# A decoder trunk on one core: the attention's matmuls in the order of the source, forget logits by token, gate biases on another queue

## The chip, the cores and the metric

The kernel runs on one core of a Trainium2 chip. The metric is the device time of one execution in microseconds, as a median over several runs. The engines that matter here: PE (TensorE, matmuls and transposes, with PEld for its weight loads), DVE (VectorE), ACT (ScalarE), POOL (GpSimd) and SP (SyncE, which does no arithmetic here and issues nearly all transfers). PSUM holds what PE writes.

## The reference

The inputs are x (256 tokens x 1024, float32), a conditioning vector c and the parameters. There are two layers. Layer 0 mixes tokens with an S5 state space, layer 1 with attention that has a forget gate per head; each is followed by a mixture of experts (32 experts in 4 groups, the top 2 of one group). Every part begins with an RMS norm and a shift and a gain worked out from c, and is added back through a gate worked out from c:

```python
def shared_kv(x, c, ...):                  # after layer 0
    h = modulate(rmsnorm(x, kv_g), shift, scale)
    k, v, fz = jnp.split(h @ kv_w, [D_MODEL, 2 * D_MODEL], axis=-1)   # fz: 16 forget logits a token
    k = rmsnorm(k.reshape(bsz, seq, N_HEADS, HEAD_DIM), k_norm_g).transpose(0, 2, 1, 3)
    logf = jax.nn.log_sigmoid(fz + kv_fb)
    fcum = jnp.cumsum(logf, axis=1).transpose(0, 2, 1)

def fox_mixer(h, w_qg, q_norm_g, w_o, k, v, fcum):
    q, og = jnp.split(h @ w_qg, 2, axis=-1)          # og: the output gate
    q = rmsnorm(q ...)
    logits = einsum(qb, kb) * scale + fcum[:, :, s0:s1, None] - fcum[:, :, None, :s1]
    p = softmax(where(causal mask, logits, NEG))     # in two blocks of 128 queries
    return (o * jax.nn.sigmoid(og)) @ w_o

# layer l:  h = h + gate * mix(...);  h = h + gate * hier_moe(...)
```

## The kernel before

**Stages.** The S5 layer runs until about 206 us, the experts of layer 0 (MoE0) until 424, the attention until about 640, and the experts of layer 1 (MoE1) to the end at 852. All weights are float32 and come from memory once, in blocks of 1 MB (128 partitions x 2048). `block` takes a block, and `prefetch` issues transfers ahead of use into a ring of slots, in an order that the source sets; a block is issued on SP's queue when the slot's last reader is done. In the attention the ring has 12 slots; `release` and the end of the values add 3 and 4 slots out of memory that the heads gave up, and MoE1's first blocks are fetched into all 19 (`ahead_of_moe`, `load`).

**Projections.** k, v and q are projections of the normed and modulated x (`hn_parts`: 16 transposes L1156, shift and gain on ACT and DVE into xf, then xf split into a hi and a lo part). A weight block of 512 columns is split likewise (`split_next`: hi on ACT at L1128, lo on DVE at L1129, tile ws, three buffers). `project` does six matmuls per quarter (hi x hi, lo x hi, hi x lo for two token halves, L1199), 48 per projection; a run of two gives k, v or q. `out_gate` (L1393, 12 a quarter, 192 in all) forms the output gate and `out_proj` (L1430, 96) the output.

**Fillers.** Shift, gain and gate for the attention are worked out from c by PE (`ada_cols_pe`, L169; `ada_gate_pe`, L184 and L194) and those for MoE1 by DVE (`ada_cols_v`, L214, one pass over 128 x 1024 at a time), in pieces that the source places between projections. POOL multiplies wo by the gate (L1126, 16 times).

**Heads.** They go in four groups. `turned_heads` transposes k and q (L1291); `weights` forms the logits of 128 queries, then of the other 128 (L1316), adds the mask and takes the maximum on DVE (L1319), negates it (L1323), takes the exponent on ACT (L1325), the reciprocal of the sum (L1327), and multiplies (L1328); `turned_weights` transposes the weights (L1342); `values` multiplies by v (L1409, L1412). These are generators, which `tick` advances between quarters.

**Forget gates.** `forget_logits` (L1189) forms the logits as 16 x 256 (head by token); `forget_gates` adds the bias, turns them by two transposes (L1243) into 128 x 32, and goes on with log-sigmoid and cumulative sum.

**Order.** The framework's scheduler orders each engine's instructions by its own costs, so PE's program isn't the source's. Each engine executes its row in order. A wait on PE holds what stands behind it.

**Lines that the change touches:** L181 (gate biases), L535 to L589 (`overflow`, which is entered only when an expert has more tokens than its tile, which isn't so with these inputs), L1173 on (the attention), L1189 and L1238 on (forget logits and gates), L1480 (the end of the attention).

Of the kernel before, what the change touches and what calls it, by code (L numbers as in the profile page):

```python
# [21 lines left out]
KD = 8  # L22
# [12 lines left out]
C_RB, C_LRE, C_LIM, C_LDT, C_GB, C_S5D, C_N = 140, 212, 244, 276, 308, 340, 356  # L35
# [3 lines left out]
def trunk(ctx: ExitStack, tc: tile.TileContext, A, out, ring=12, ring2=4, ring3=5, ring4=3, ring5=4, lpb=2, TK=2):  # L39
# [135 lines left out]
    def ada_gate_pe(name, j, li, gbc, at_once=False):  # L175
# [4 lines left out]
        for n in range(2):  # L180
            nc.scalar.dma_start(rows[32 * n:32 * n + 1, :], A["gbias"][li, n:n + 1, :])  # L181
# [150 lines left out]
    def moe(l, sh, g, gbc, c36, slots_):  # L332
# [200 lines left out]
        def overflow(rv):  # L533

            with tc.If(rv > CAP):  # L535
# [15 lines left out]
                with tc.For_i(0, NQ, 1) as q:  # L551
                    gcol = t2("gcol", 4)
                    G.dma_start(gcol, gov.rearrange("p i (q s) -> p i q s", s=4)[:, :, bass.ds(q, 1), :]
                                      .rearrange("p i o s -> p i (o s)"))
                    for s in range(4):
                        c = slice(512 * s, 512 * s + 512)

                        def part(name, j):
                            w = mb[0].tile([128, 2, 512], F32, tag="ow", name="ow", bufs=1)
                            G.dma_start(w, A[name][l, bass.ds(q, 1), 2 * j:2 * j + 2, :, c]  # L560
                                              .rearrange("o k p n -> p (o k) n"))
                            return w

                        ph = [mm_tile() for _ in range(2)]
                        for kp in range(4):
                            w = part("wa", kp)
                            for i in range(2):
                                for kk in range(2):
                                    PE.matmul(ph[i], hnT[i][:, 2 * kp + kk, :], w[:, kk],
                                              start=kp + kk == 0, stop=kp == 3 and kk == 1)  # L570
                        aTs = []
                        for i in range(2):
                            a = mb[0].tile([128, 256], F32, tag="a", name="oa", bufs=2)
                            S.activation(a, ph[i][:, 0:256], AF.Silu)
                            V.scalar_tensor_tensor(a, a, gcol[:, i, s:s + 1], ph[i][:, 256:512],
                                                   op0=OP.mult, op1=OP.mult)
                            aTs.append(turned(a))
# [1043 lines left out]
```

## Time and profile before

| what | value |
| --- | --- |
| median of 3 runs (lowest, highest) | 849.39 us (849.17, 849.5) |
| profiled execution: time, span | 854.14 us, 852.5 us |
| mean granted clock of PE | 0.941 |
| busy: PE, DVE, ACT, POOL | 722.5 (85%), 410.1 (48%), 218.3 (26%), 58.3 (7%) us |
| moved from memory | 297.31 MB, mean 350 GB/s with what is written |
| chain that ended last, by engine | PE 47%, DMA 31%, DVE 17%, ACT 2%, issue 2% |

Busy time is an average over stages with different limits: the experts' stages move weights at about 419 GB/s without a pause, while the attention is limited by what its engines do. A row in time gives the start, the length of a group of like instructions (a float32 matmul leaves two records, and some records can be missing, so xcount is a count of records), the operation with its tiles, and in brackets the idle time of the engine before it with what ended it. Lengths of neighbouring PE rows overlap a little, since matmuls are pipelined.

### The profile page before, as it was taken

How to read it: one execution, taken by the hardware profiler on the slowest of the kernel's cores; microseconds unless marked ns; L12 is line 12 of the kernel's file. 1: busy time of each engine (PE TensorE's matmuls, PEld its weight loads, DVE VectorE, ACT ScalarE, POOL GpSimd, SP SyncE). 2: the span in 40 equal slices, each digit the busy share in tenths (PEclk: the TensorE clock that was granted, in tenths of full speed). 3: DMA queues.
4: the chain of work that ended last, by engine and by line, in shares of the span. 5: the costliest groups of instructions: out<-in, count | busy, mean ns of one | idle time of the engine just before them, and what ended most of it. 6: DMA issues, size and time to landing. Idle time of an engine off the chain costs nothing.

```text
span 852.5 us, 13440 instructions
## 1 busy us (share of the span) xinstructions
PE 722.5 (85%) x5382; PEld 401.3 (47%) x5382; DVE 410.1 (48%) x1069; ACT 218.3 (26%) x498; POOL 58.3 (7%) x52
## 2 busy tenths in 40 slices
PE   2777999898899997576799999899998999887766
PEld 0655776575533333131255567788755334331311
DVE  6657799875322322120355569997553223221102
ACT  4323233162300110010232255556522001100100
POOL 2000000000000000000001202870000000000000
PEclk9988999998999999889799999999989999997898
DMA  9996856687999999999999787552679999999996
GB/s 365 416 420 256 328 218 248 264 344 289 419 420 418 421 418 419 420 416 421 420 418 399 282 324 260 196 188 100 241 306 394 419 419 419 418 419 419 418 418 247
DMA packets 41830, 299.32 MB, mean 351 GB/s; under 512 B 4632, under 2 KB 4760, under 8 KB 5664
## 3 DMA queue, kind: packets, MB, share of 16 engines
q1 hardware_dynamic: 41328, 297.13, 86.3%
q10 hardware_dynamic: 432, 1.25, 0.4%
q8 instruction: 45, 0.74, 0.4%
q14 instruction: 25, 0.20, 0.1%
HBM read 297.31 MB, written 1.05 MB: 350 GB/s over the span
## 4 chain that ended last, share of the span: by engine, by line
PE 47%; DMA 31%; DVE 17%; ACT 2%; issue 2%; POOL 0%; SPq 0%; ACTq 0%; DVEq 0%; POOLq 0%
DMA w<-wa 14%; DMA w<-wb 10%; PE mm L506 8%; PE acc L1199 7%; PE mm L470 5%; PE mm L521 4%; PE acc L528 4%; PE acc L1430 3%; DVE m L921 2%; DMA w<-win 2%; DVE m L935 2%; DMA w<-ada00g 2%; PE mm L169 2%; DMA w<-ada 2%; DVE m L954 2%; PE acc L1393 2%
## 5 line engine op out<-in xcount | busy, mean ns | idle before, releaser
L506 PE MATMUL mm<-w,xg 128*32 128x512 f32 x1024 | 140.0, 637 | 33.6 <-DMA w<-wa 22.7
L506 PEld LDWEIGHTS mm<-w,xg 128*32 128x32 f32 x1024 | 29.4, 111 | 118.3 <-issue 69.1
L521 PE MATMUL mm<-w,aT 128*32 128x512 f32 x512 | 68.4, 650 | 12.1 <-DMA w<-wb 6.3
L1199 PE MATMUL acc<-ws,hn 128*128 128x512 f32 x288 | 77.7, 409 | 0.7 <-DVE ws L1129 0.7
L478 ACT ACTIVATE xg<-mm,sh,g 128x128 f32<-128x128 f32 x64 | 29.3, 457 | 187.0 <-PE mm L470 170.9
L1129 DVE TENSOR_TENSOR ws<-w,ws 128x512 fp32r<-128x512 f32 x80 | 60.7, 768 | 32.7 <-ACT ws L1128 32.5
L470 PE MATMUL mm<-Pr,h 128*128 128x128 f32 x512 | 64.9, 280 | 11.0 <-DVE Pr L458 11.0
L470 PEld LDWEIGHTS mm<-Pr,h 128*128 128x128 f32 x512 | 60.5, 193 | 26.4 <-issue 23.2
L528 PE MATMUL acc<-y,Sc 128*128 128x512 f32 x128 | 64.7, 629 | 6.5 <-DVE y L524 5.7
L1128 ACT ACTIVATE ws<-w 128x512 fp32r<-128x512 f32 x80 | 49.7, 629 | 67.9 <-PE acc L1199 49.5
L476 DVE TENSOR_SCALAR xg<-mm,g,sh 128x128 f32<-128x128 f32 x64 | 26.2, 410 | 75.2 <-ACT xg L478 75.2
L1199 PEld LDWEIGHTS acc<-ws,hn 128*128 128x128 f32 x288 | 51.1, 188 | 23.9 <-issue 7.1
L524 DVE TENSOR_TENSOR y<-mm,gbc 128x512 f32<-128x512 f32 x32 | 22.1, 692 | 67.6 <-PE mm L521 67.3
L489 DVE COPY Sc<-mm 128x256 f32<-128x256 f32 x16 | 6.8, 425 | 86.0 <-PE mm L487 86.0
L511 ACT ACTIVATE a<-mm 128x256 f32<-128x256 f32 x16 | 6.1, 383 | 163.7 <-PE mm L506 163.7
L528 PEld LDWEIGHTS acc<-y,Sc 128*128 128x128 f32 x128 | 22.2, 193 | 45.9 <-issue 28.7
L512 DVE TENSOR_TENSOR a<-a,mm 128x256 f32<-128x256 f32 x16 | 6.7, 419 | 76.9 <-ACT a L511 76.9
L521 PEld LDWEIGHTS mm<-w,aT 128*32 128x32 f32 x512 | 14.1, 114 | 53.6 <-issue 35.4
L984 PE MATMUL acc<-w,uT 128*128 128x512 f32 x64 | 31.7, 642 | 5.7 <-ACT uT L973 5.7
L808 PE MATMUL mm<-hnT,w 128*64 128x128 f32 x512 | 33.3, 291 | 2.7 <-ACT hnT L275 2.7
L1393 PE MATMUL acc<-hn,ws 128*128 128x256 f32 x192 | 29.4, 310 | 5.2 <-DVE ws L1129 5.2
L808 PEld LDWEIGHTS mm<-hnT,w 128*64 128x64 f32 x512 | 31.4, 143 | 4.5 <-ACT hnT L275 3.7
(337 smaller groups left out, 1004.2 us busy)
## 6 DMA issues: line engine op xcount, KB each, us to landing
w<-wa SPq DMA_DIRECT2D x128, 1024.0 KB, 19.9
w<-wb SPq DMA_DIRECT2D x64, 1024.0 KB, 19.9
w<-ada SPq DMA_DIRECT2D x36, 1024.0 KB, 8.8
w<-ada00s SPq DMA_DIRECT2D x8, 1024.0 KB, 18.0
w<-kvada SPq DMA_DIRECT2D x8, 1024.0 KB, 9.1
w<-win SPq DMA_DIRECT2D x4, 1024.0 KB, 18.5
w<-ada00g SPq DMA_DIRECT2D x4, 1024.0 KB, 18.9
w<-woutv SPq DMA_DIRECT2D x4, 1024.0 KB, 17.4
```

The costliest lines, as they stand in the source:

```text
L470: PE.matmul(px[:, 128 * c4:128 * c4 + 128], h[:, i, 128 * c:128 * c + 128], Pr[:, i].rearrange("p a b -> p (a b)"), start=i == 0, stop=i == 1)
L476: V.tensor_scalar(xg[:, c], src, g[:, c:c + 1], sh[:, c:c + 1], op0=OP.mult, op1=OP.add)
L478: S.activation(xg[:, c], src, AF.Identity, bias=sh[:, c:c + 1], scale=g[:, c:c + 1])
L506: PE.matmul(ph[32 * s:32 * s + 32, :], xg[:, k, 32 * s:32 * s + 32], w[:, 512 * s:512 * s + 512], start=k == 0, stop=k == KD - 1)
L521: PE.matmul(py[32 * s:32 * s + 32, :], aT[:, 128 * f + 32 * s:128 * f + 32 * s + 32], w[:, 512 * s:512 * s + 512], start=f == 0, stop=f == 1)
L528: PE.matmul(acc[i][n], scs[q][:, 128 * i:128 * i + 128], y[:, 512 * n:512 * n + 512], start=q == 0, stop=q == NQ - 1, skip_group_check=True)
L808: PE.matmul(ps[64 * v:64 * v + 64, 128 * hh:128 * hh + 128], w[:, k, c0:c0 + 64], hnT[:, k, v::2], start=k == 0 and hh == 0, stop=k == KD ...
L984: PE.matmul(val[t][n], uT[:, m, 128 * t:128 * t + 128], wval[m // 2][:, c0:c0 + 512], start=m == 0, stop=m == 7)
L1128: S.activation(o[:, 0], w, AF.Copy)
L1129: V.tensor_tensor(o[:, 1], w, o[:, 0].bitcast(F32), op=OP.subtract)
L1199: PE.matmul(pk[i], src[:, k, a, 128 * i:128 * i + 128], w[:, b], start=k + a + b == 0, stop=k == KD - 1 and b == 1)
L1393: PE.matmul(po[:, 256 * m2:256 * m2 + 256], w[:, bb, kk, 128 * m2:128 * m2 + 128], hq[:, k, a, :], start=k + a + bb + m2 == 0, stop=k == K ...
```

## The change

1. In `ada_gate_pe` the two transfers of the gate's bias (2 KB each, four gates) are issued by SP and not by ACT.
2. From the norm of x for k and v to the end of the attention PE's instructions keep the order of the source (`manual_schedule`); the other engines' rows are still the scheduler's.
3. The forget logits are formed by token: x is the stationary operand (128 x 128) and the 16 columns of weights the moving one, 16 matmuls for 8 before. The result is 128 x 32 at once; zT, the two transposes and a copy go, and the bias comes as 32 columns.
4. `overflow` has a second hardware loop in place of a Python loop over four quarters; its weights come by SP, its gates are shifted by two copies. The scratch for dynamic transfers is 1024 and not 2048.

```diff
@@ ada_gate_pe
-            nc.scalar.dma_start(rows[32 * n:32 * n + 1, :], A["gbias"][li, n:n + 1, :])
+            nc.sync.dma_start(rows[32 * n:32 * n + 1, :], A["gbias"][li, n:n + 1, :])
@@ overflow
-                with tc.For_i(0, NQ, 1) as q:
-                    gcol = t2("gcol", 4)
-                    G.dma_start(gcol, ...)
-                    for s in range(4):
-                        c = slice(512 * s, 512 * s + 512)
+                gnext = t2("gnext", NE)
+                with tc.For_i(0, NQ, 1) as q, tc.For_i(0, 2048, 512) as c:
...
+                    V.tensor_copy(gnext[:, :, 0:NE - 1], gov[:, :, 1:NE])
+                    V.tensor_copy(gov[:, :, 0:NE - 1], gnext[:, :, 0:NE - 1])
...
@@ the attention
+    in_order = ExitStack()
+    in_order.enter_context(tc.manual_schedule(engines={PE.engine}))
     xs = tp.tile([128, 2, D], F32, tag="xs", name="xs", bufs=1)
@@ forget_logits
-            PE.matmul(pz[:16, :T], smallw[:, k, 0:16], x[:, k2, :], start=k == 0, stop=k == KD - 1)
+            for i in range(2):
+                PE.matmul(pz[:, 16 * i:16 * i + 16], x[:, k2, 128 * i:128 * i + 128], smallw[:, k, 0:16],
+                          start=k + i == 0, stop=k == KD - 1, skip_group_check=True)
@@ forget_gates
-        zT = ap.tile([16, T], F32, name="zT")
-        V.tensor_scalar(zT, pz[:16, :T], cols[:16, C_FB:C_FB + 1], None, op0=OP.add)
-        yield
-        pt = mm_tile()
-        for i in range(2):
-            PE.transpose(pt[:, 16 * i:16 * i + 16], zT[:, 128 * i:128 * i + 128], ident[:16, :16])
...
-        V.tensor_copy(fz, pt[:, :32])
+        V.tensor_tensor(fz, pz[:, 0:32], cols[:, C_FBR:C_FBR + 32], op=OP.add)
@@ end of the attention
     out_proj(3)
+    in_order.close()
     ssq = new_ssq()
...
-    nc = bacc.Bacc("TRN2", target_bir_lowering=False, num_devices=1, dynamic_dma_scratch_size=2048)
+    nc = bacc.Bacc("TRN2", target_bir_lowering=False, num_devices=1, dynamic_dma_scratch_size=1024)
```

Three places of the engines' rows. In the changed kernel L1200 is what L1199 was, L1153 was L1156, L1285 was L1291, L1310 was L1316, L1336 was L1342, L1387 was L1393, L1126 was L1129, L1226 was L1225, L1317 was L1323, L1321 was L1327, L1322 was L1328 and L1409 was L1415; L1189 and L169 keep their numbers. A number x16 counts instructions.

PE where k begins, before (the shift's columns L169, the logits L1189, the projection L1199):

```order
L169 MATMUL mm<-w,sc 32x256 x13
L1189 MATMUL acc<-xf,smallw 16x256
L1199 MATMUL acc<-ws,hn 128x512 x2
L169 MATMUL mm<-w,sc 32x256 x3
L1199 MATMUL acc<-ws,hn 128x512 x5
L1189 MATMUL acc<-xf,smallw 16x256
L1199 MATMUL acc<-ws,hn 128x512 x4
L1189 MATMUL acc<-xf,smallw 16x256
L1199 MATMUL acc<-ws,hn 128x512 x6
L1189 MATMUL acc<-xf,smallw 16x256
L1199 MATMUL acc<-ws,hn 128x512
L1189 MATMUL acc<-xf,smallw 16x256
```

The same place after, from the transposes of x to the cumulative sum of the forget gates (`tri`) and the rest of the fourth projection:

```order
L1153 MATMUL mm<-ident,xs 128x128 x16
L1189 MATMUL acc<-smallw,xf 128x16 x16
L1200 MATMUL acc<-ws,hn 128x512 x48
L169 MATMUL mm<-w,sc 32x256 x32
L1200 MATMUL acc<-ws,hn 128x512 x48
L169 MATMUL mm<-w,sc 32x256 x32
L1200 MATMUL acc<-ws,hn 128x512 x6
L1263 MATMUL mm<-f_z,tri 128x16
L1264 MATMUL mm<-f_z,ones 128x16
L1265 MATMUL mm<-f_z,tri 128x16
L1200 MATMUL acc<-ws,hn 128x512 x42
```

The columns stand in two blocks of 32, each behind 48 projections, where they were spread in pieces between them; the logits stand ahead of the first projection.

PE at the first head group, before, from the logits of the heads (L1316) over the output gate (L1393) to the first turned weights (L1342):

```order
L1316 MATMUL mm<-kA,qA 128x128 x4
L1393 MATMUL acc<-hn,ws 128x256 x2
L1199 MATMUL acc<-ws,hn 128x512 x2
L1393 MATMUL acc<-hn,ws 128x256 x22
L1316 MATMUL mm<-kA,qA 128x256 x4
L1393 MATMUL acc<-hn,ws 128x256 x4
L1291 MATMUL mm<-ident,kn 66x128 x4
L1393 MATMUL acc<-hn,ws 128x256 x48
L1342 MATMUL mm<-ident,pr 128x128 x4
L1291 MATMUL mm<-ident,kn 66x128 x4
```

The same place after (L1310, L1387, L1336):

```order
L1387 MATMUL acc<-hn,ws 128x256 x12
L1310 MATMUL mm<-kA,qA 128x128 x4
L1387 MATMUL acc<-hn,ws 128x256 x12
L1310 MATMUL mm<-kA,qA 128x256 x4
L1387 MATMUL acc<-hn,ws 128x256 x36
L1285 MATMUL mm<-ident,kn 66x128 x4
L1336 MATMUL mm<-ident,pr 128x128 x4
```

Of the output gate's matmuls 76 stood between the first logits and the first turned weights, and now 48; 12 now stand ahead of the logits.

DVE ahead of the first group's multiply by the reciprocal, before (L1328; L214 is a pass over a weight block for MoE1, L1129 the split of a block):

```order
L1221 TENSOR_SCALAR ss<-ss 128x8
L1327 RECIPROCAL sm<-sm 128x4
L214 ISA w,g_111<-w,scr 128x1024
L214 ISA g_111 128x1
L214 ISA w,g_111<-w,scr 128x1024
L214 ISA g_111 128x1
L1129 TENSOR_TENSOR ws<-w,ws 128x512
L1323 TENSOR_SCALAR mx<-mx 128x4
L1328 TENSOR_TENSOR pr<-pr,sm 128x512
```

The same stretch after, up to L1322:

```order
L1317 TENSOR_SCALAR mx<-mx 128x4
L1226 TENSOR_TENSOR qn<-acc,rs 128x8x64
L1126 TENSOR_TENSOR ws<-w,ws 128x512
L1317 TENSOR_SCALAR mx<-mx 128x4
L1409 TENSOR_SCALAR sgT<-sgT 128x512
L1126 TENSOR_TENSOR ws<-w,ws 128x512
L214 ISA w,g_111<-w,scr 128x1024
L214 ISA g_111 128x1
L214 ISA w,g_111<-w,scr 128x1024
L214 ISA g_111 128x1
L1321 RECIPROCAL sm<-sm 128x4
L1126 TENSOR_TENSOR ws<-w,ws 128x512
L217 TENSOR_TENSOR g_111<-g_111,cols 128x8
L1322 TENSOR_TENSOR pr<-pr,sm 128x512
```

The two L1226, which write q's heads, and two more splits stand ahead of the multiply; in before the same L1225 stood behind it.

## Rows read from the trace of the kernel before

**Rows 1.** Windows: from:to, length, busy (instructions) by engine, clock, DMA, GB/s.

```profile
424.00:450.00 26.00, 22.58 (x129) 12.28 (x128) 14.23 (x25) 9.86 (x19) 2.06 (x2) 0.93 1.01 419
...
450.00:480.00 30.00, 30.00 (x148) 15.33 (x147) 18.51 (x61) 9.56 (x17) 4.69 (x4) 1.00 0.88 350
...
480.00:510.00 30.00, 30.00 (x140) 18.60 (x140) 16.52 (x31) 12.15 (x21) 2.86 (x2) 1.00 0.89 326
...
530.00:560.00 30.00, 24.01 (x146) 21.21 (x146) 30.00 (x52) 15.53 (x35) 26.08 (x16) 0.91 0.55 200
```

**Rows 2.** Chain of waits, end of the span: start, length, what.

```profile
732.67 19.89 DMA w<-wb
...
813.80 20.11 DMA w<-wa
```

**Rows 3.** PE in time: start, length, operation, records, idle before.

```profile
428.64 1.97 PE L1156 MATMUL mm<-ident,xs 128*128 128x128 f32 x8 [0.93 <-DVE xs L254]
...
432.12 2.08 PE L169 MATMUL mm<-w,sc 128*32 128x256 f32 x23
...
480.29 1.18 PE L1199 MATMUL acc<-ws,hn 128*128 128x512 f32 x4
...
495.34 1.06 PE L184 MATMUL mm<-w,sc 128*32 128x512 f32 x8
...
515.51 16.11 PE L1199 MATMUL acc<-ws,hn 128*128 128x512 f32 x68
...
626.81 2.77 PE L382 MATMUL acc<-smallw,hT 128*128 128x36 f32 x24
...
633.08 5.22 PE L184 MATMUL acc<-w,sc 128*32 128x512 f32 x32
```

**Rows 4.** Chain of waits, the gate columns before the S5 layer.

```profile
86.08 3.59 PE mm L169 x64
```

**Rows 5.** DVE in time, projections.

```profile
431.21 1.29 DVE L1168 TENSOR_TENSOR hn<-xf,hn 128x512 fp32r<-128x512 f32 x2 [0.24 <-ACT hn L1167]
...
435.27 0.54 DVE L1163 TENSOR_SCALAR xf<-mm,gkv,shkv 128x256 f32<-128x256 f32 x1 [0.66 <-ACT xf L1165]
...
508.75 1.22 DVE L214 CUSTOM_DVE_ANT_0 w<-w,scr 128x1024 f32<-128x1024 f32 x1
```

**Rows 6.** PE in time, head groups.

```profile
536.39 1.06 PE L1316 MATMUL mm<-kA,qA 66*128 66x128 f32 x8
...
538.00 2.77 PE L1393 MATMUL acc<-hn,ws 128*128 128x256 f32 x22
...
540.60 1.89 PE L1316 MATMUL mm<-kA,qA 66*128 66x256 f32 x8
...
546.34 5.57 PE L1393 MATMUL acc<-hn,ws 128*128 128x256 f32 x32 [2.46 <-DVE ws L1129]
...
554.38 0.66 PE L1342 MATMUL mm<-ident,pr 128*128 128x128 f32 x4
...
557.47 6.04 PE L1393 MATMUL acc<-hn,ws 128*128 128x256 f32 x36 [2.00 <-DVE ws L1129]
...
565.21 1.16 PE L1316 MATMUL mm<-kA,qA 66*128 66x128 f32 x8
```

**Rows 7.** DVE in time, head groups.

```profile
531.09 3.31 DVE L1129 TENSOR_TENSOR ws<-w,ws 128x512 fp32r<-128x512 f32 x2
...
553.65 0.68 DVE L1328 TENSOR_TENSOR pr<-pr,sm 128x512 f32<-128x512 f32 x1
...
573.85 0.69 DVE L1328 TENSOR_TENSOR pr<-pr,sm 128x512 f32<-128x512 f32 x1
```

**Rows 8.** POOL in time.

```profile
530.88 14.19 POOL L1126 TENSOR_TENSOR w<-w,gbc 128x512 f32<-128x512 f32 x8
```

**Rows 9.** The tile rows: engine, operation, ns min/median/max, first to last start.

```profile
L179 POOL MEMSET rows<- x4: 524/524/527, 30.0 to 632.3; 128x512 f32 x4
```

**Rows 10.** Waits of the SP queue, 553 to 660 us: total, times, longest.

```profile
SPq L67 <- PE acc L184: 12.7, 3, 11.1
```

More of the change, by code (lines that the diff above doesn't have):

```diff
@@ new lines, in overflow, with part @@
+                with tc.For_i(0, NQ, 1) as q, tc.For_i(0, 2048, 512) as c:
+                    def part(name, j):
+                        w = mb[0].tile([128, 2, 512], F32, tag="ow", name="ow", bufs=1)
+                        nc.sync.dma_start(w, A[name][l, bass.ds(q, 1), 2 * j:2 * j + 2, :, bass.ds(c, 512)]
+                                          .rearrange("o k p n -> p (o k) n"))
+                        return w
+                    ph = [mm_tile() for _ in range(2)]
+                    for kp in range(4):
+                        w = part("wa", kp)
+                        for i in range(2):
+                            for kk in range(2):
+                                PE.matmul(ph[i], hnT[i][:, 2 * kp + kk, :], w[:, kk],
+                                          start=kp + kk == 0, stop=kp == 3 and kk == 1)
+                    aTs = []
+                    for i in range(2):
+                        a = mb[0].tile([128, 256], F32, tag="a", name="oa", bufs=2)
+                        S.activation(a, ph[i][:, 0:256], AF.Silu)
+                        V.scalar_tensor_tensor(a, a, gov[:, i, 0:1], ph[i][:, 256:512], op0=OP.mult, op1=OP.mult)
+                        aTs.append(turned(a))
+                    V.tensor_copy(gnext[:, :, 0:NE - 1], gov[:, :, 1:NE])
+                    V.tensor_copy(gov[:, :, 0:NE - 1], gnext[:, :, 0:NE - 1])
+                    for n in range(2):
+                        w = part("wb", n)
+                        py = [mm_tile() for _ in range(2)]
+                        for f in range(2):
@@ L567, in overflow @@
                             for i in range(2):
[L568 to L571, printed above, removed]
+                                PE.matmul(py[i], aTs[i][:, 128 * f:128 * f + 128], w[:, f],
+                                          start=f == 0, stop=f == 1)
                         for i in range(2):
[L573 to L577, printed above, removed]
@@ L578, in overflow @@
[L578 to L592 removed]
+                            for c2 in range(2):
+                                r = slice(256 * c2, 256 * c2 + 256)
+                                t = mb[0].tile([128, 256], F32, tag="a", name="ot", bufs=2)
+                                V.tensor_tensor(t, py[i][:, r], gbc[:, 512 * n + 256 * c2:512 * n + 256 * c2 + 256],
+                                                op=OP.mult)
+                                PE.matmul(acc[i][n][:, r], ident, t, start=False, stop=False, skip_group_check=True)
@@ L1188, in forget_logits @@
             k = 2 * kk + k2
-            PE.matmul(pz[:16, :T], smallw[:, k, 0:16], x[:, k2, :], start=k == 0, stop=k == KD - 1)
+            for i in range(2):
+                PE.matmul(pz[:, 16 * i:16 * i + 16], x[:, k2, 128 * i:128 * i + 128], smallw[:, k, 0:16],
+                          start=k + i == 0, stop=k == KD - 1, skip_group_check=True)
     hk = hn_parts(xs, shkv, gkv, forget_logits)
@@ L1540, in layouts @@
     cols[:64, C_QG] = fox_q_norm_g[0]
-    for j in range(4):
-        cols[:, C_GB + 8 * j:C_GB + 8 * j + 8] = col(ab[j, 2 * D:])
+    cols[:, C_FBR:C_FBR + 32] = np.tile(np.asarray(kv_fb), 2)[None]
     kvw = np.asarray(kv_w)
```

28 lines of the change are left out of this document (1 added, 27 removed).

## The prediction

> **What bounds the kernel now.** I read the windows first, then the end of the chain of waits, then PE's instructions in time through the attention, and last what DVE and POOL do where PE idles. The end of the span is a stream of weights: five transfers of about 20 us follow each other in the chain until 833.9 us [rows 2], so MoE1 ends when its blocks have landed. A 1 MB block costs about 2.5 us of that stream (eight queue inside one 19.89). Of MoE1's 96 blocks, 19 have slots before it starts; the other 77 x 2.5 = 192 us can only begin when its first matmuls free slots. So a microsecond won or lost ahead of MoE1 is one at the end. What counts is the attention, 424 to 640 us. There PE is busy throughout the projections (30.00 of 30 us in two windows) and DVE is busy throughout 530 to 560, where PE has 24.01 of 30 [rows 1].
>
> **The change part by part.**
>
> *k, v and their fillers.* Before, the 128 records of the shift and gain columns (L169) stand in some 25 pieces between the projections, ends at 480.29 [rows 3]. After, PE does all forget logits, then 48 projections, 32 columns, 48, 32, 48. The bunched form has its own row: 64 records in 3.59 us [rows 4], so 7.2 for both halves. A projection in a long run takes 16.11/68 = 0.237 us [rows 3], so the 108 that before has done by 480.29 take 25.6. The three small matmuls of the cumulative sum add 0.6. The start: the logits now keep the first projection behind the fourth pair of columns of x. DVE formed that pair by 435.27 + 0.54 = 435.8 [rows 5], and the last eight records of the logits come after it at 2.77/24 = 0.115 each (L382 [rows 3]), 0.9 us: 436.7 at the latest. ScalarE's part of it stood behind a run of 23 L169 that began at 432.12 and took 2.08 [rows 3], which is no longer there; at the earliest 435.3. I take 436.0. New wait: DVE does two passes of L214 (1.22 each [rows 5]) ahead of the fifth split, and PE has nothing else in its row by then: up to 2.4, I take 2.3. The end is 436.0 + 25.6 + 7.2 + 0.6 + 2.3 = 471.7 against 480.3: **-8.6**. Bounds: -10 (start at 435.3, half of the wait) to -5 (further waits for ws of 0.2 us on each of 18 splits). The 16 logits themselves are no term: 32 records at 0.115 are 3.7 us, inside the time in which x's columns are formed. The dropped transposes, zT and its copy lie beside other work, worth 0.2 on PE.
>
> *The gate and the second set of transposes.* Six pieces of L184 (1.06 with eight records, some of it under the next operation [rows 3]; I count 1.0) become one bunch; the bunch has a row of 5.22 [rows 3], so 6.0 becomes 5.2, -0.8. The transposes for q, before spread among projections, now stand together ahead of q: PE waits from its last transpose until the first hi and lo exist. For k the transposes ended at 428.64 + 1.97 = 430.6 [rows 3], and DVE had the first two lo parts at 431.21 + 1.29 = 432.5 [rows 5]: 1.3 to 1.9 us for one or both, and with two L214 ahead on DVE 3.7 to 4.3. I take 2.4, nearer to the first since the L214 may be done by then: net **+1.6**, bounds +0.5 to +3.5.
>
> *q.* 96 projections in the same form; DVE has no slack here, more waits on ws: **+0.7**, bounds 0 to +2.5.
>
> *The first head group.* This is the place that decides. In before PE issues the first logits of heads (L1316) at 536.39, and L1342, which turns the weights, at 554.38 [rows 6], because DVE's L1328 runs at 553.65 [rows 7]. In between PE does 76 of the 192 gate projections L1393, and still idles 2.46 us in one piece [rows 6]. After, only 48 stand between the two, and 12 ahead. Cover after: L1316 1.06 and 1.89, 48 x 0.118 = 5.7 (22 in the 2.60 from 538.00 to 540.60), and about 0.5 for four transposes (0.66 for those at 554.38): 9.1 us [rows 6]. DVE's chain was 553.65 + 0.68 - 536.39 = 17.9 us long [rows 6, 7]. PE therefore stands about **9 us in one piece**. Most of it isn't lost against before, since before was held by the same chain; lost is what PE did meanwhile: 16 L1393, 1.9 us. Besides, the order on DVE puts three splits, two L1225 and L214 differently: two L1225 and a split stand ahead of L1328 now that stood behind it, and the backlog of splits and L214 before L1319 is longer; 0 to 5 us, I take 3. Against that, before waited 2.00 at 557.47 for just this work [rows 6], which goes. Net **+2.9**, bounds 0 to +7.
>
> The trace shows POOL's eight multiplies of wo from 530.88 [rows 8], and beside them two splits (L1129) taking 3.31 us [rows 7], where two subtractions of the same size take 1.29 [rows 5]; after, both stand in the same stretch of the order. The Trainium skill (SBUF — State Buffer, Who interferes with whom) says that a DVE instruction with two inputs in SBUF contends with a GpSimd instruction that reads SBUF. By that, the chain is as long in after; without it, the stall would be 2.0 shorter with each such pair.
>
> In the 2.46 us of idle before 546.34 PE waited for ws, and what stands behind in its row waited with it [rows 6]; so nothing behind L1342 fills the 9 us. The Trainium skill (TensorE: Matmul & The Clock Gate, Step-by-step: what each phase is for) says that matmuls stay in program order and only weight loads are pulled ahead. By that the 9 us stay empty, as the row has it; if PE could pass the wait, the sum would be 1.9 us better.
>
> *The other groups.* Group 1: chain from 565.21 [rows 6] to 573.85 + 0.69 [rows 7], 9.3 us; cover in after: 1.1 + 1.9 for L1316, 36 L1393 at 0.118 = 4.2, 1.6 for the values' 16 records (estimated at the 0.1 of small matmuls) and 0.5: 9.3; no stall to speak of. Group 2 has 12 L1393 fewer behind the values, 7.9, so 1.4 if its chain is as long; group 3 has 24 output matmuls at 0.237 and is covered. A part of that was idle before too: **+0.7**, bounds -1 to +4. The granted clock was 0.91 in 530 to 560, where PE idled 6 us [rows 1]; a single longer idle may cost as much again, 0.09 x 30 = 2.7, or nothing: **+0.5**.
>
> *gbias on SP.* The two 2 KB transfers wait for POOL's memset of rows, first at 30.0 and last at 632.3 us [rows 9]. SP's next block in MoE1 waits up to 11.1 us for L184 anyway, which begins at 633.08 [rows 3, 10]. With SP blocked, what it would hold up is the weights behind; about eight blocks are in flight (19.89 for one of 2.5 us [rows 2]). **0**, bounds -0.3 to +2.
>
> *overflow, the scratch size.* The block isn't entered; its branches lie in the end of each MoE, under the DMA stream. **0**, bounds -1 to +1.
>
> Sum: -8.6 + 1.6 + 0.7 + 2.9 + 0.7 + 0.5 = **-2.2**. The profiled execution takes 854.14 us (span 852.5), 4.75 above the median of 849.39; I apply the same difference to both, so 851.9 profiled and **847.2** for the median.
>
> **The rivals.**
>
> *The whole lead stays.* DVE is as far ahead as PE, because its splits are made at PE's pace and the L1225 moved forward aren't missing later. Then the first group costs 0 and the small terms 0: -8.6 + 1.6 = -7.0, with the lower bounds of both -9.5: 842.4 to 839.9. For it: DVE is busy only 18.51 of 30 in the projections [rows 1]. Against it: 30.00 of 30 between 530 and 560.
>
> *Nothing stays: the weights aren't there.* From 424 to 510 the windows move 26 x 419 + 30 x 350 + 30 x 326 = 31.2 MB [rows 1], 74.4 us at 419 GB/s. After has about 79 us for it, so DMA would be at 94%. If blocks come in the wrong order for it, some 2 to 3 us of the lead become waits: -2.2 + 2.5 = +0.3, 848 to 851. Against it: blocks are issued up to 12 slots ahead.
>
> *Slower: each head group stalls.* The mechanism is that of the first group: with PE in source order each chain L1319, exponent, L1328 is covered only by the 7 to 9 us of work that the source places in it. It decides from the point where the chains of groups 1 to 3 average above about 10 us, which needs DVE as late there as in the first group. At 13 us: 3 x 13 - (9.3 + 7.9 + 9.5) = 12 us of stalls, 11 more than counted, and 2 back since the splits are then ready: -2.2 + 9 = +6.8, 856.2. With 11 us each, 33 - 26.7 = 6.3, 5 more than counted, +2.8, 852.2. For it: POOL's second eight multiplies fall beside group 1. Against it: the chain of group 1 is 9.3 us as traced.
>
> **How the numbers follow.** Forecast (842 to 850) 0.52, of which 0.44 lies below 847.7; the whole lead 0.14; nothing stays 0.14; slower 0.20. What a measurement can tell from no change is 0.2%, 1.7 us. Faster: 0.44 and the whole lead's 0.14 give 0.58; the forecast's edge of 0.08 and the third case give 0.22 for the same; slower 0.20. The range reaches from 839.5, where the second case ends, to 854.5, halfway between the slower case's two prices; the forecast's own is 842 to 850.
>
> **What would show it.** Right: PE's 32 columns in one piece of 3.6 us, k and v done near 472, one idle of 7 to 12 us ahead of the first turning of weights, released by DVE's last multiply by the reciprocal; MoE1's first gather 2 to 3 us earlier. Wrong: idle of several us ahead of that operation in each group, or idle in the projections released by DMA, or a first gather no earlier. If SP's gbias issue stands waiting while later blocks' slots are free, that term is wrong.

## The result, and the profile after

The changed kernel takes 837.39 us (835.78 to 839.52, 4 runs) against 849.44 for the kernel before (849.17 to 850.22, 4 runs): 12.0 us less, ratio 0.9858, 95% interval 0.9829 to 0.9887. In a later comparison on one chip it took 838.88 (6 runs) against 849.27 (17 runs), ratio 0.9872 (0.9842 to 0.9901). The forecast was 847.2 with a range from 839.5 to 854.5. The sign was right; the size was far off, and the time lies below the range.

The traced execution took 838.87 us, span 837.1. Since before's traced execution lay 4.75 above its median and this one 1.5, the two traces differ by 15.3 us where the medians differ by 12.0. All places below are taken from traces, so some 3 us of what they show is the two executions and not the change. Of the changed kernel's four executions two had a mean granted clock of 0.930 and 0.932 and took 839.52 and 838.87 us, two had 0.942 and 0.945 and took 835.91 and 835.78; the traced one is of the first pair.

| place in the traces, us from the start | before | after | after less before |
| --- | --- | --- | --- |
| MoE0's first gather | 212.64 | 204.42 | -8.2 |
| first transpose of x for k | 426.65 | 417.61 | -9.0 |
| first projection | 434.56 | 427.79 | -6.8 |
| first turned weights of heads | 554.38 | 545.99 | -8.4 |
| first transpose for MoE1 | 624.62 | 610.52 | -14.1 |
| MoE1's first gather | 639.74 | 624.70 | -15.0 |
| span | 852.5 | 837.1 | -15.4 |

A gather (L470) is the operation with which PE collects the tokens of four experts; with the first one an MoE's work on its experts begins. So some 9 of the 15 us were there before the attention had begun, in a part of the program for which the forecast had a zero. From the attention on, MoE1 behaves as forecast: what is won ahead of its first gather is won at the end.

**Ahead of the attention.** ACT's and PE's rows in time in the kernel before, around the bias transfers of the first gate (`rows`), which ACT issued:

```profile
30.54 1.93 ACT L275 ACTIVATE hnT<-acc,sh,g 128x256 f32<-128x256 f32 x4 [4.27 <-DVE g L155]
...
46.35 2.67 ACTq L181 DMA_DIRECT2D rows<-gbias  x2
...
49.06 0.51 ACT L855 ACTIVATE ab<-braw 128x128 f32<-128x128 f32 x2 [16.59 <-DMA w<-ada00g]
```

```profile
49.42 1.12 PE L864 MATMUL mm<-ident,ab 128*128 128x128 f32 x4 [5.56 <-ACT ab L855]
...
51.32 2.08 PE L916 MATMUL mm<-uT,bz 128*128 128x128 f32 x8 [0.18 <-ACT bz L867]
```

ACT has nothing to do but issue two transfers of 2 KB from 32.5 on, and stands 16.59 us (the 2.67 of the two issues lie in it), released by the landing of a 1 MB block of ada00g. ACT's row in order, with the semaphores that each instruction waits for; Pool_49 is the memset of `rows`, which the bias needs, but DMAHW1 and DMAHW2 have nothing to do with its data:

```
L181 DMA rows<-gbias 1x512 [waits DMAHW1_49,Pool_49]
L181 DMA rows<-gbias 1x512 [waits DMAHW2_49]
L855 ACTIVATE ab<-braw 128x2x64 [waits DMAHW4_49]
```

The program gives the transfers of SP and ACT eight such semaphores in turn, whichever of the two issues them, and in SP's row the third and fourth ada00g block have the same two (DMAHW1, DMAHW2). So the bias waits until they have landed, and L855 behind it on ACT, which prepares the S5 layer's b, waits as well; then PE idles 5.56 us, and its next operations run slowly (2.08 us for eight records; the granted clock is 0.52 from 49 to 56 us, and 1.00 from 43 to 50 in the changed kernel). ACT, PE and SP at the same place after:

```profile
34.42 0.51 ACT L852 ACTIVATE ab<-braw 128x128 f32<-128x128 f32 x2 [2.33 <-DMA braw<-s5b]
...
44.26 1.27 ACT L864 ACTIVATE bz<-mm,half 128x512 f32<-128x512 f32 x2 [0.19 <-PE mm L861]
```

```profile
43.56 0.66 PE L861 MATMUL mm<-ident,ab 128*128 128x128 f32 x4
...
45.00 1.16 PE L913 MATMUL mm<-uT,bz 128*128 128x128 f32 x8 [0.38 <-ACT bz L864]
```

```profile
46.01 2.67 SPq L181 DMA_DIRECT2D rows<-gbias  x2
...
51.00 2.96 SPq L67 DMA_DIRECT2D w<-ada  x2
```

L852 (L855 before) is done at 34.9 and not at 49.6, PE has no idle ahead of L861, and the same eight records take 1.16. SP issues the bias at 46.01, just when ACT did, and its next block at 51.00, where before it was 51.32: SP was waiting for the same landings anyway.

**The attention.** The windows that answer to [rows 1], in the same columns; the program is some 9 us ahead in them:

```profile
424.00:450.00 26.00, 26.00 (x151) 20.38 (x152) 19.73 (x61) 9.12 (x16) 3.26 (x2) 0.82 0.97 387
...
450.00:480.00 30.00, 30.00 (x197) 20.96 (x196) 16.76 (x32) 11.94 (x20) 3.73 (x3) 1.00 1.01 413
...
480.00:510.00 30.00, 27.69 (x117) 21.54 (x117) 23.98 (x42) 17.35 (x30) 1.25 (x1) 0.94 0.85 331
...
530.00:560.00 30.00, 17.74 (x134) 16.62 (x134) 24.77 (x64) 14.26 (x39) 14.66 (x9) 0.77 0.37 140
```

PE's row in time, which answers to [rows 3, 6]:

```profile
427.79 14.07 PE L1200 MATMUL acc<-ws,hn 128*128 128x512 f32 x48
...
441.79 3.66 PE L169 MATMUL mm<-w,sc 128*32 128x256 f32 x64
...
456.78 3.66 PE L169 MATMUL mm<-w,sc 128*32 128x256 f32 x64
...
462.45 10.04 PE L1200 MATMUL acc<-ws,hn 128*128 128x512 f32 x42
...
472.42 3.64 PE L184 MATMUL mm<-w,sc 128*32 128x512 f32 x32
...
491.51 13.01 PE L1200 MATMUL acc<-ws,hn 128*128 128x512 f32 x48 [2.31 <-ACT hn L1164]
...
518.92 0.72 PE L1387 MATMUL acc<-hn,ws 128*128 128x256 f32 x4
...
523.97 1.91 PE L1310 MATMUL mm<-kA,qA 66*128 66x128 f32 x8
...
545.99 1.09 PE L1336 MATMUL mm<-ident,pr 128*128 128x128 f32 x4 [12.26 <-issue]
...
610.52 0.60 PE L353 MATMUL mm<-ident,h 128*128 128x128 f32 x4
```

The columns (L169) stand in two pieces of 3.66, the gate (L184) in one of 3.64, q waits 2.31 for hi and lo, and the first turned weights (L1336) come after one idle of 12.26. For its end the row says `issue`: the profile shows no releaser. DVE's multiply L1322, which writes what L1336 reads, ends at 545.21 + 0.68 = 545.89 (its row stands further down). All that is as forecast in kind. Two things are not. The first 48 projections take 14.07, where the next 48 take 11.46, and the first window shows a granted clock of 0.82. And the 12.26 us at the heads are followed by a run with hardly any idle up to 610.52.

### The profile page after: what moved, and what is told of

Its sections match the earlier page's. It is cut to its first block, busy times and chain, and to the rows that moved or that the text cites. A ratio compares the mean times of both kernels' runs of the same rounds, so it can differ in the third digit from the quotient of the medians.

```text
span 837.1 us, 13449 instructions
## 1 busy us (share of the span) xinstructions
PE 710.3 (85%) x5396; PEld 407.1 (49%) x5396; DVE 412.0 (49%) x1068; ACT 218.8 (26%) x498; POOL 51.8 (6%) x52
## 5 line engine op out<-in xcount | busy, mean ns | idle before, releaser
L506 PE MATMUL mm<-w,xg 128*32 128x512 f32 x1024 | 144.3, 645 | 28.7 <-DMA w<-wa 10.9
L1200 PE MATMUL acc<-ws,hn 128*128 128x512 f32 x288 | 74.2, 416 | 2.3 <-ACT hn L1164 2.3
L1126 DVE TENSOR_TENSOR ws<-w,ws 128x512 fp32r<-128x512 f32 x80 | 60.9, 765 | 29.6 <-ACT ws L1125 29.3
L470 PE MATMUL mm<-Pr,h 128*128 128x128 f32 x512 | 64.2, 279 | 11.2 <-DVE Pr L458 11.2
L470 PEld LDWEIGHTS mm<-Pr,h 128*128 128x128 f32 x512 | 59.8, 192 | 26.0 <-issue 18.6
L1200 PEld LDWEIGHTS acc<-ws,hn 128*128 128x128 f32 x288 | 56.4, 199 | 18.1 <-ACT hn L1164 2.5
L521 PEld LDWEIGHTS mm<-w,aT 128*32 128x32 f32 x512 | 14.1, 113 | 53.0 <-issue 37.1
L1387 PE MATMUL acc<-hn,ws 128*128 128x256 f32 x192 | 28.5, 303 | 2.6 <-DVE ws L1126 2.6
```

Source lines behind the costliest of these rows:

```text
L470: PE.matmul(px[:, 128 * c4:128 * c4 + 128], h[:, i, 128 * c:128 * c + 128], Pr[:, i].rearrange("p a b -> p (a b)"), start=i == 0, stop=i == 1)
L506: PE.matmul(ph[32 * s:32 * s + 32, :], xg[:, k, 32 * s:32 * s + 32], w[:, 512 * s:512 * s + 512], start=k == 0, stop=k == KD - 1)
L521: PE.matmul(py[32 * s:32 * s + 32, :], aT[:, 128 * f + 32 * s:128 * f + 32 * s + 32], w[:, 512 * s:512 * s + 512], start=f == 0, stop=f == 1)
L1126: V.tensor_tensor(o[:, 1], w, o[:, 0].bitcast(F32), op=OP.subtract)
L1200: PE.matmul(pk[i], src[:, k, a, 128 * i:128 * i + 128], w[:, b], start=k + a + b == 0, stop=k == KD - 1 and b == 1)
L1387: PE.matmul(po[:, 256 * m2:256 * m2 + 256], w[:, bb, kk, 128 * m2:128 * m2 + 128], hq[:, k, a, :], start=k + a + bb + m2 == 0, stop=k == K ...
```

## The experiments

All times are medians, compared with the kernel before on the same chip; the ratio is not the quotient of the two medians, and its 95% interval is in brackets. The runs e1 to e4, e5 to e8, e9 to e12 and e13 were on four different chips, so between these groups the ratios are compared. One of e12's 12 executions took 1762.74 us; its ratio leaves that out.

| run | time, us | before, us | ratio |
| --- | --- | --- | --- |
| e1_gbias_first | 845.43 | 849.34 | 0.9945 [0.9922, 0.9968] |
| e2_order_only | 843.46 | 849.34 | 0.9921 [0.9893, 0.9948] |
| e3_gbias_back | 843.95 | 849.34 | 0.9930 [0.9907, 0.9952] |
| e4_order_proj | 839.36 | 849.34 | 0.9880 [0.9851, 0.9908] |
| e5_gbias_order | 837.28 | 849.06 | 0.9858 [0.9833, 0.9884] |
| e6_turn_later | 840.60 | 849.06 | 0.9904 [0.9880, 0.9927] |
| e7_gbias_pool | 843.44 | 849.06 | 0.9927 [0.9903, 0.9952] |
| e8_overflow_only | 847.92 | 849.06 | 0.9983 [0.9961, 1.0005] |
| e9_after_again | 838.88 | 849.27 | 0.9872 [0.9842, 0.9901] |
| e10_head_logits | 836.24 | 849.27 | 0.9839 [0.9809, 0.9868] |
| e11_columns_between | 836.26 | 849.27 | 0.9848 [0.9815, 0.9880] |
| e12_forget_only | 851.03 | 849.27 | 0.9996 [0.9971, 1.0021] |
| e13_passes_moved | 838.77 | 848.89 | 0.9865 [0.9839, 0.9892] |

**Bias transfers: e1, e3, e7.**

```diff
 e1, on before:   -nc.scalar.dma_start(rows...)   +(nc.sync if li == 0 else nc.scalar).dma_start(rows...)
 e7, on before:   -nc.scalar.dma_start(rows...)   +(nc.gpsimd if li == 0 else nc.scalar).dma_start(rows...)
 e3, on after:    -nc.sync.dma_start(rows...)     +nc.scalar.dma_start(rows...)
```

> Kernel before, with only the first gate's two bias transfers (S5 layer) issued by SP; the other three gates stay on ACT. Theory A (the gain ahead of the attention is ACT's: in the trace of before ACT issues these two only after it has stood 16.6 us for the landing of an ada00g block, so the copies of u that PE needs come 5.6 us and more late): 8.3 us faster, 841.1, ACT's 16.6 us wait gone, MoE0's first gather at 204.4 in place of 212.6. Rival B (the gain is from MoE0's end or from another part of the change, such as the shorter skipped block): within 1 us of before.

> Kernel before, with the first gate's two bias transfers issued by POOL. Theory A (what counts is that ACT doesn't stand for a transfer's lane): as e1_gbias_first, MoE0's first gather near 205, 843.5 to 846. Rival B (it is something that SP's queue does, such as the order of transfers in its queue): MoE0's first gather at 212, 848 to 850.

> Changed kernel with the eight bias transfers issued by ACT again. Theory A: the 16.6 us wait of ACT is back and 8.3 us with it, 845.7. Rival B (SP only removes a wait that would be hidden): 837 to 839.

In e1's trace MoE0's first gather is at 205.72, in e7's at 205.24 and in e3's at 213.90, so theory A holds for the place: two 2 KB transfers of one gate, taken off ACT, make the S5 layer some 7 us shorter, and it doesn't matter which other queue they go to. Over all 15 traces that gather comes at 211.8 to 213.9 where ACT issues the bias and at 204.1 to 206.6 where SP or POOL does. ACT in e7, where POOL issues them:

```profile
34.70 0.51 ACT L855 ACTIVATE ab<-braw 128x128 f32<-128x128 f32 x2 [2.34 <-DMA braw<-s5b]
```

The same line that stood at 49.06 before. The times move by less than theory A said: 4.7 us by e1's ratio (2.7 to 6.6), 6.2 by e7's, and e3 is 5.1 us above the changed kernel in e9's comparison (6.6 above the first one). The S5 layer's gain is 6.9 and 7.4 us in the traces of e1 and e7; in e1's it arrives whole at the end (span 845.7 for 852.5), but before's traced execution was itself 4.75 above its median. Whether a part of the gain doesn't reach the time stays open, since e1's interval lies below 6.9 and e7's (4.1 to 8.2) holds 7.4. The six transfers of the other three gates were not tried by themselves.

**The order: e2, e4, e5.**

```diff
 e2, on before:               e4, on after:                   e5: e2 with all bias transfers on SP
+    in_order.enter_context(   +    in_order.close()
+        tc.manual_schedule(       out_gate(0)
+        engines={PE.engine}))  ...
     xs = tp.tile(...)              out_proj(3)
 ...                           -    in_order.close()
     out_proj(3)
+    in_order.close()
```

> Kernel before, with PE in source order through the attention and nothing else. Theory A (the order is worth what the attention got shorter by in the trace of the changed kernel, 6.0 us from the first transpose of x to MoE1's first gather, less 0 to 2 for the logits by token): 4 to 6 us faster, 844 to 845.5. Rival B (PE's order is worth about nothing, as forecast -2.2 and the logits do the rest): 847 to 850. In both one idle of PE of 9 us or more ahead of the first turned weights.

> Changed kernel with the source order ended ahead of the output gate, so that PE's row from there on is the scheduler's. Theory A (the idle of 12.3 us ahead of the first turned weights is a loss that the scheduler's order avoids): 3 to 8 us faster than the changed kernel, 830 to 834. Rival B (the idle only moves work: DVE is ahead afterwards and PE catches up, as the changed kernel does from 546 to 610 us): 836 to 840.

> Kernel before with the eight bias transfers on SP and PE in source order through the attention; forget logits by head as before and the overflow block as before. Theory A (the logits by token cost about 2.4 us where the projections begin, since PE now waits in order for them; the overflow block nothing): 835, 2 us faster than the changed kernel, first projection 7.9 us after the first transpose of x in place of 10.2. Rival B (logits by token are a gain as well): 838 to 841.

From the first transpose of x to MoE1's first gather, with PE in the scheduler's order: 213.1 us in before and in e1, 210.5 in e7, 210.1 in e8. In the source's order with logits by head: 204.4 in e2, 203.2 in e5, 203.4 in e10; with logits by token 207.1 in the changed kernel, 206.8 in e9, 206.4 in e3. So with logits by head the order is worth 6 to 10 us in traces, and 5.9 in e2's time (6.7 by its ratio, 4.4 to 9.1): theory A, at its upper end or a little above. e5, at 837.28, lies between its two theories, and its ratio is the changed kernel's first one.

The gain is in PE's own work. From the first transpose of x to MoE1's first gather PE is busy 201.0 of the 213.1 us in before and 184.0 of the 204.4 in e2: 17 us less work, and 8.4 us more idle. The largest single part is the columns (L169) over that stretch, spread in pieces in before and in two blocks in e2; the numbers behind the bar are their busy time in us and the mean of one record in ns:

```profile
L169 PE MATMUL mm<-w,sc 128*32 128x256 f32 x128 | 17.1, 388 | 0.0
```

```profile
L169 PE MATMUL mm<-w,sc 128*32 128x256 f32 x128 | 7.3, 380 | 0.0
```

The 288 records of the projections take 77.7 in before and 73.4 in e2. e4 has the source's order in the projections alone, and takes 208.9 us in the stretch and 839.36 in all, as the changed kernel does within the intervals: its theory A falls, and most of the order's gain is there already with k, v, the gate and q. What e4's PE waits for from 515 us on, in part:

```profile
520.44 4.33 PE L1387 MATMUL acc<-hn,ws 128*128 128x256 f32 x22 [1.70 <-DVE ws L1126]
...
532.69 1.21 PE L1387 MATMUL acc<-hn,ws 128*128 128x256 f32 x8 [3.62 <-DVE ws L1126]
...
534.38 2.93 PE L1387 MATMUL acc<-hn,ws 128*128 128x256 f32 x12 [0.48 <-DVE ws L1126]
```

With five more waits of 0.4 to 2.0 us it is 10.9 us in pieces. The changed kernel has 15.5 from there on (2.56, 12.26 and 0.69): the scheduler's order there has some 4.5 us less idle, but from the first transpose of x to MoE1's first gather e4's PE is busy 192.4 us for 186.3, so nothing is gained by it.

**The first head group: e6, e13.**

```diff
 e6, on e5, in turned_weights:               e13, on e10:
+        for _ in range(4 if hg == 0 else 0):  -    VP = [9, 9, 4, 3]
+            yield                             +    VP = [9, 6, 99, 2]
```

> The kernel of the run e5_gbias_order, with the first group's turning of weights four turns later in the source, so that 36 more output gate matmuls (about 4.3 us) and eight transposes stand ahead of it. Theory A (the 12 us idle ahead of the turned weights only moves work, since DVE is the bound until it ends): within 1.5 us of e5_gbias_order, the idle shorter by 4 to 6 us, and as much lost in waits for ws or behind. Rival B (the idle is a loss to PE): 4 us faster than e5_gbias_order.

> The kernel of e10_head_logits, with DVE's passes for MoE1's shift and gain (L214) taken out of the turns of q and the output gate and put into the turns of v and of the output projection, so that no pass stands between the first group's maximum (L1318) and its multiply (L1327). Theory A (the 10.3 us idle ahead of the first turned weights is partly those passes, 2.28 and 2.27 us in the trace of the changed kernel, and the idle moves work, so PE has to do it all the same later): idle shorter by 4 to 5 us, time 2 to 4 us below e10_head_logits, ratio to before 0.979 to 0.982. Rival B (as with e6_turn_later, what is taken away from this wait comes back in others, since DVE is busy without a pause there): within 1.5 us of e10_head_logits, ratio 0.982 to 0.986.

DVE in the changed kernel, between the first group's maximum (L1313) and its multiply (L1322):

```profile
530.16 0.28 DVE L1313 CUSTOM_DVE_ANT_0 pr<-mm,mask 128x128 f32<-128x128 f32 x1
...
539.06 2.28 DVE L214 CUSTOM_DVE_ANT_0 w<-w,scr 128x1024 f32<-128x1024 f32 x1
...
541.27 2.27 DVE L214 CUSTOM_DVE_ANT_0 w<-w,scr 128x1024 f32<-128x1024 f32 x1
...
543.56 1.65 DVE L1126 TENSOR_TENSOR ws<-w,ws 128x512 fp32r<-128x512 f32 x1
...
545.21 0.68 DVE L1322 TENSOR_TENSOR pr<-pr,sm 128x512 f32<-128x512 f32 x1
```

DVE has no idle from 519 to 547. Beside POOL's multiplies of wo a pass L214 takes 2.28 and a split 1.65 (1.22 and 0.69 at 507 us, ahead of them), and these stand ahead of L1322 on DVE. In e6 more of PE's work stands ahead of the turned weights; PE's waits there:

```profile
540.96 2.08 PE L1397 MATMUL acc<-hn,ws 128*128 128x256 f32 x8 [5.12 <-DVE ws L1129]
...
561.70 0.63 PE L1346 MATMUL mm<-ident,pr 128*128 128x128 f32 x4 [2.02 <-ACT ws L1128]
...
579.52 2.06 PE L1434 MATMUL acc<-ws,oT 128*128 128x512 f32 x5 [1.10 <-DVE oT L1426]
```

The long wait is now for ws and half as long as e5's (5.12 for 10.24), there are new ones behind, and the time is 3.3 us above e5. From the first transpose of x to MoE1's first gather PE idles 21.5 us (e5 21.0) and is busy 186.3 (e5 182.1): the idle moved, and PE's own work took 4.2 us more. In e13 no pass stands in the stretch (VP sets after how many turns a pass is made, with a number for each run of turns); PE's waits:

```profile
466.55 0.58 PE L1268 MATMUL mm<-f_z,tri 128*128 128x16 f32 x2 [5.71 <-DVE f_z L1265]
...
531.27 1.06 PE L1290 MATMUL mm<-ident,qn 128*66 128x128 f32 x4 [6.77 <-DVE qn L1224]
...
543.66 4.15 PE L1392 MATMUL acc<-hn,ws 128*128 128x256 f32 x20 [3.17 <-DVE ws L1126]
...
548.63 0.63 PE L1341 MATMUL mm<-ident,pr 128*128 128x128 f32 x4 [0.37 <-ACT pr L1324]
```

The one of 10.3 us is gone (0.37 is left). Ahead of it the wait for the forget gates, which now stand behind more passes on DVE, has grown from 3.44 in e10 to 5.71, 6.77 for q's heads is new, and the one for ws is 3.17 for 0.67. In all PE idles 22.9 us from the first transpose of x to MoE1's first gather, in e10 21.1. e13's ratio is 0.0026 above e10's, with intervals that overlap. So in both, the idle that was taken away came back elsewhere. e6 fits neither theory, being slower than both had it; e13 fits rival B in kind, at 0.9865 just outside its range. That fits with DVE being the bound from 515 to 545 us, where it is busy 30.00 of 30 in the changed kernel, e10 and e13; that it is the bound was not shown by making it faster. Whether a smaller load on DVE (without the slowing beside POOL) would help wasn't tried.

**The logits: e9, e10, e11, e12.**

```diff
 e10, on after (e12 is the opposite, on before):
-            for i in range(2):
-                PE.matmul(pz[:, 16*i:16*i+16], x[:, k2, 128*i:128*i+128], smallw[:, k, 0:16], ...)
+            PE.matmul(pz[:16, :T], smallw[:, k, 0:16], x[:, k2, :], ...)
 e11, on e10, in forget_logits:
+        if kk == 0:
+            step(ada)          # 32 column matmuls; the step behind k's first half is left out
```

> The changed kernel itself, for a comparison on one chip with the next two. 836 to 839; in its trace the granted clock is 0.50 from the logits by token to some 5 us into the first projections, as in the first trace (421 to 433 us).

> Changed kernel with the forget logits by head (16 x 256) again; bias transfers, source order and overflow block as changed. Theory A (logits by token keep PE at the lower of its two clock levels: 6.85 us for them against 4.42, and 14.1 us for the first 48 projections against 11.4): first projection 8.2 us after the first transpose of x in place of 10.2, first 48 in 11.5 us, 3 to 4.5 us faster than the changed kernel, 833 to 834.5. Rival B (what is won there is lost in the wait of the first head group, which DVE ends): within 1.5 us of the changed kernel.

> The kernel of e10_head_logits with the first 32 column matmuls (L169) between the first and the second pair of logits, where PE waits for x, and not behind 48 projections. Theory A (PE has idle there that the scheduler's order of before filled with just this): 1 to 3 us faster than e10_head_logits. Rival B (weights: the four blocks for it now come ahead of wk, and the first projection waits for its splits): 0 to 4 us slower than it.

> Kernel before, with forget logits by token and nothing else; PE's row is the scheduler's. Theory A (PE's other work stands between the logits there, so that the clock rises as before): within 1.5 us of before. Rival B (the lower clock level as in the changed kernel): 2 to 4 us slower than before.

The logits in the changed kernel: PE, PE's weight loads, and the windows of the same stretch and the next:

```profile
421.11 6.85 PE L1189 MATMUL acc<-smallw,xf 128*128 128x16 f32 x32
```

```profile
420.89 6.95 PEld L1189 LDWEIGHTS acc<-smallw,xf 128*128 128x128 f32 x32
```

```profile
421.00:433.00 12.00, 12.00 (x46) 10.90 (x45) 8.56 (x27) 4.16 (x8) 0.00 (x0) 0.50 1.01 417
...
433.00:450.00 17.00, 17.00 (x121) 12.48 (x120) 13.67 (x39) 6.78 (x12) 3.26 (x2) 0.98 0.95 370
```

The same in e10, PE and windows:

```profile
422.88 4.69 PE L1188 MATMUL acc<-xf,smallw 128*16 128x256 f32 x16
...
427.49 11.45 PE L1198 MATMUL acc<-ws,hn 128*128 128x512 f32 x48
```

```profile
422.00:428.00 6.00, 6.00 (x23) 2.50 (x22) 4.45 (x8) 4.15 (x8) 0.00 (x0) 0.76 1.01 415
...
428.00:440.00 12.00, 12.00 (x71) 9.15 (x74) 8.25 (x15) 5.68 (x10) 0.00 (x0) 1.00 1.01 419
```

PE is busy 12.00 of 12 us in both kernels, yet with the logits by token the granted clock stays at 0.50, the lower of the two levels (1.2 GHz), from 421 to 433 us: through the 6.85 us of logits and some 5 us into the projections. With 256 moving columns it rises to 1.00 before the first projection. e9's trace repeats the changed kernel's (0.50 from 421 to 432, 6.85 for the logits, 13.74 for the first 48 projections). Price in place: 6.85 against 4.69 for the logits, and 14.07 against 11.45 for the projections, 4.8 us.

The Trainium skill (TensorE: Matmul & The Clock Gate, LDWEIGHTS (loading the stationary operand)) says that a weight load's time goes by the columns of the stationary operand; by its formula, columns / 1.2, an estimate for 128 is 107 ns. The trace agrees at the upper level (L382 of before, 24 loads of 128 columns in 2.76 us, 115 ns each). At the lower level it has 6.95/32 = 217 ns, about twice that: PE spends this stretch loading weights, 128 columns for every 16 that move.

These 4.8 us are not what e10 gains at the end. The same places, from the first transpose of x in each trace:

| us from the first transpose of x to | e9 | e10 |
| --- | --- | --- |
| first projection | 10.5 | 8.3 |
| end of the first 48 projections | 24.2 | 19.8 |
| q's first projection | 73.9 | 74.3 |
| first turned weights | 128.2 | 124.4 |
| MoE1's first gather | 206.8 | 203.4 |

When q begins the lead of 4.4 us is gone. Most of it goes in a wait of the cumulative sum for the forget gates, which DVE forms and which have zT, the two transposes and a copy in their way again; the changed kernel has no wait there:

```profile
464.37 0.37 PE L1268 MATMUL mm<-f_z,tri 128*128 128x16 f32 x2 [3.44 <-DVE f_z L1265]
```

A lead of 3.9 us comes only between q and the first turned weights, the stretch that DVE ends. From the first transpose of x to there DVE is busy 100.5 us in e9 and 97.3 in e10, with 200 and 199 instructions; why is not shown. In time e10 is 2.6 us below e9, between its two theories. So the price of the lower clock is shown in place, and not that it is what e10 gains.

e12 shows no difference from before by its ratio, within theory A's range, but its trace contradicts the reason that theory A gives. The scheduler puts L169 between the logits, and the clock doesn't rise:

```profile
430.00:450.00 20.00, 20.00 (x85) 15.05 (x84) 8.77 (x17) 5.85 (x10) 0.00 (x0) 0.50 0.90 370
```

In before the granted clock is 0.96 in that window. The traced execution took 858.80 us, the longest of e12 but the one left out, so how often this happens is open. e11 gains nothing on e10. Its PE is 2.2 us ahead of e10 when q begins (72.1 for 74.3 from the first transpose), the wait for the forget gates is the same 3.44, and at the first turned weights it is 1.5 behind (125.9 for 124.4), again in the stretch that DVE ends. e10_head_logits, the change without its logits by token, has the lowest median of these, 836.24, but e11 (836.26) and e5 can't be told from it; it is 0.3% below e9, whose low end (837.61) lies within its range, as do the changed kernel's two shorter executions (835.78 and 835.91). The gain over the changed kernel is at the edge of what these runs tell.

**The overflow block: e8.**

```diff
 e8, on after:  bias on ACT, no in_order, logits by head; the new overflow block and the scratch of 1024 stay
```

> Changed kernel with the bias transfers on ACT, the scheduler's order on PE and the forget logits by head: only the overflow block and the scratch size differ from before. Theory A: within 1.5 us of before. Rival B (the shorter skipped code is read faster by the queues and ends each MoE earlier): 2 us or more faster, MoE0 shorter than 214 us.

0.9983, with 1 within the interval, which reaches from 3.3 us faster to 0.4 slower. MoE0 takes 213.2 us in its trace against 214.0, but it takes 210.5 to 214.6 over the 15 traces, so that tells nothing. The block is worth a few us at most; a small gain as in rival B is not excluded.

## Why the prediction was right and wrong

The step that failed first is the one called *gbias on SP*: **0**, bounds -0.3 to +2. Its argument went only through what SP might lose. What ACT would be rid of wasn't looked for, though the trace of before showed it without any change: an idle of 16.59 us ahead of an ACT instruction, released by a DMA that this instruction doesn't read, and 5.56 us on PE behind it. [rows 9] have the memset that the first issue needs at 30.0, and the issue came at 46.35. That is 4.7 to 6.6 us in time (e1, e7, e3), more than the whole of the forecast's 2.2. The bound that was to exclude a gain had no reason behind it.

The second is the sum of the attention: -2.2 was forecast, and it is -6.0 in the traces against before's 213.1 us (-3.0 against the 210.1 of e8, which has the same order). In time e3, the change without its bias transfers, is 5.4 us below before, and e2, the order alone, 5.9. Most of the difference in the table is the term for the gate and q, +2.3 for -1.0.

The terms from the first transpose of x in each trace; the first stretch ends when 108 projections are done, the second at the first operation of the head group:

| stretch | forecast | in the traces |
| --- | --- | --- |
| k, v, columns, cumulative sum | -8.6 | -7.4 |
| gate, second transposes, q | +1.6 and +0.7 | -1.0 |
| first head group, to its turned weights | +2.9 | +9.1, with 16 L1393 (1.9) still to do |
| other groups, to MoE1's first transpose | +0.7, clock +0.5 | -5.7 |
| to MoE1's first gather | 0 | -0.9 |
| sum | -2.2 | -6.0 |

*k, v.* Near its size, but by errors against each other, which is luck. The start was put 9.4 us behind the first transpose (436.0 in before's time); it came 10.2 behind it, and the first 48 projections cost 2.6 more at the lower clock. Against that, the wait of 2.3 ahead of the fifth split didn't come: PE has no idle from 424 to 480. "The 16 logits themselves are no term" was wrong: they were counted at 0.115 us a record, a rate that was read at the upper level. What they cost in the end is open (e10 above). The bunching of L169 was priced rightly: 3.66 twice, for 3.6.

*Gate and q.* The wait for hi and lo was 2.31 for 2.4, L184 took 3.64 for 5.2 (the row it was read from, 5.22, ran at a granted clock of 0.67), and the waits on ws for which +0.7 stood didn't come, while before's own 0.9 and 0.7 went. Against that, q's first 48 projections took 13.01 for 11.46, at a granted clock of 0.87.

*Heads.* One idle ahead of the turned weights, of 12.26 for 9, as said, and nothing behind it in PE's row filled it. Its net cost at that point was put at +2.9 and was three times that; but the rest then ran 5.7 us faster with more to do. From the first turned weights to MoE1's first gather PE idles 2.7 us in the changed kernel and 6.3 in before (where 2.00 of it is for a split), and it is busy 76.0 for 79.1: the values' work is no longer cut into single records between other matmuls. Together the head terms are +3.4 for the forecast's +4.1: the sum was near, its division wasn't, and that is luck too. The forecast treated the idle as lost on PE. In the rows PE waits for no split from 546 to 610, so DVE had used the time to get ahead with ws.

The rivals: that each head group stalls was wrong, groups 1 to 3 have one wait of 0.69 us. That weights would lack was wrong too; in 450 to 480 the transfers ran at 413 GB/s without PE waiting for one. "The whole lead stays" had nearly the right size for the attention (-7.0 for -6.0) for a wrong reason: the first group was to cost 0, and cost 9.1. None of the cases had a part ahead of 424 us.

## What to carry to other kernels

A transfer that a compute engine issued stood in that engine's row here like any instruction, and held what came behind it for 16.59 us, though it was 2 KB and nobody needed it soon: look in the trace for an idle of the engine that ends with the landing of a foreign block, and put small transfers on the queue of an engine that has nothing to do then (SP or POOL here). When an edit moves work from A to B, price what A is rid of with the same care as what B gets. Like matmuls in one run can be worth a wait: the same 128 records of L169 took 7.3 us in two blocks and 17.1 in pieces. And when an edit changes the shape of a matmul, read the granted clock of the stretch behind it too, and then follow the lead to the end: here 4.8 us won at one place were gone before q began.

## What was not expected of the hardware

In the changed kernel PE was busy without a gap and still at the lower clock: 12.00 of 12 us busy at 0.50, in 6.85 of them with matmuls that move 16 columns for every 128 loaded and then some 5 us with projections, which in e10 ran at 1.00 (14.07 against 11.45 us for 48). An idle of 5.56 us on PE in the S5 layer cost more than itself: at a granted clock of 0.52 behind it, L916 and L808 took 2.08 and 2.40 us for 1.16 and 1.35 in the changed kernel, so 5.9 us of lead at 44 us were 8.5 at the output projection (78.03 against 69.57).
